# First adaLN columns of a hybrid decoder layer: sums kept in PSUM, wider loads of w_ada, the first gate products in three parts

## The chip, the cores and the metric

The kernel runs on one core of a Trainium2 chip. The core has TensorE (matrix products, PE in the profile), VectorE (DVE), ScalarE (ACT), GpSimd (POOL) and SyncE (SP, which here issues the DMAs), a scratch memory SBUF, and PSUM, the memory that TensorE writes into. The metric is the device time of one execution in microseconds, as the median of several runs.

## The reference

One decoder layer for 1024 tokens of width 1024, in float32. A conditioning vector c gives six vectors (adaLN), the first two of which shift and scale the normed input; the result h is projected, and the projection feeds everything that follows.

```python
mod = jnp.dot(jax.nn.silu(c), w_ada) + b_ada
shift1, scale1, gate1, shift2, scale2, gate2 = [m[:, None, :] for m in jnp.split(mod, 6, axis=-1)]
h = _rmsnorm(x, norm1_w) * (1.0 + scale1) + shift1
proj = jnp.dot(h, w_in)        # queries, keys, values, indexer, retention, two gates ga and gb
...                            # sparse attention and retention, merged by the gates; FFN; last norm
merged = jax.nn.sigmoid(ga) * y_a + jax.nn.sigmoid(gb) * y_r
```

w_ada is 1024 x 6144, w_in is 1024 x 7240, x is 1024 x 1024.

## The kernel before

Every product in float32 is made of three products on TensorE: each operand is split into a high part (rounded to float32r) and a low part (the rest), and high x high, high x low and low x high are added up in PSUM. For a weight, ScalarE makes the high part (`whi`, line 77) and GpSimd the low part (`wlo`, line 80) out of the loaded tile (`graw` or `wraw`).

What the change touches is the **start** of the kernel, about its first 80 us, up to line 321. It works on column blocks of 128, of which there are eight (`KT`), numbered j, and on the first 512 of the 1024 tokens (half 0). For a block j:

1. `load_wa(j)` (line 242) loads the 128 columns j of shift1 and the 128 of scale1 out of w_ada, as two DMAs of 512 KB, into `wa` (three buffers). Each piece that lies together in memory has 128 floats, that is 512 bytes. `rows_slot` (line 95) loads and splits the two tiles `graw` of gb weights that block j needs (six buffers).
2. `start_mod(j)` (line 287) multiplies by silu(c) and adds up over the eight row tiles k, on VectorE: one `tensor_scalar` (line 296) and seven `scalar_tensor_tensor` (line 298), each over 256 columns, which all read and write `acc` in SBUF. Two products with a column of ones (line 302, two instructions each in the trace) add over the partitions into a PSUM tile `mp`, and VectorE makes the two columns `modc` from it (lines 303 and 304).
3. `make_h(j, 0)` (line 272) turns the normed x into columns by four transposes on TensorE (line 275) into a PSUM tile `tp`; ScalarE makes `hT_hi` and `hx` from it with `modc` as scale and bias (line 279), and GpSimd `hT_lo` (line 280).
4. 18 products of 128x512 on TensorE: six PSUM tiles of gb (`gb_ps`) times three kinds (lines 136, 138 and 140: whi x hT_hi, whi x hT_lo, wlo x hT_hi).

PSUM tiles `mp` and `tp` come from one pool of two (`ps_tr`, line 210). Before all that, `norm_x` (line 233) norms each tile of x: a square with a sum on ScalarE (line 236), a power on GpSimd (line 186) and a multiplication on VectorE (line 238), four tiles at the beginning and four, of the second half of the tokens, later. After the eight blocks follow `make_h` for the second half of the tokens, the stores of the gate, and at line 377 eight tiles of the indexer's key weights (`wraw`, 292 columns), whose product with all of hT is the first work that needs all eight blocks (line 123, 128x292).

The instructions of an engine run in the order in which they stand in its queue, each when what it waits for has come. A scheduler makes that order from the program; `turns_after` and `add_manual_dep` add an order to it. SP's queue of DMA issues is kept in order too, so a load that waits for its buffer holds up those behind it.

## Time and profile before

| | us |
|---|---|
| runs (three) | 1731.92, 1732.92, 1734.29 |
| median | 1732.92 |
| the profiled execution: its span, from first to last instruction | 1733.6 |
| TensorE busy in it | 1686.5 (97%) |
| TensorE busy from 0 to 20.5 us | 3.12 |
| TensorE busy from 20.5 to 81.4 us | 50.84 of 60.9 |
| first product of the indexer's keys (line 123) | at 81.45 |

No time beside the span is given for the profiled execution; the span lies between the runs. In the profile an engine's row in the timeline has the start, the duration, engine, line, operation, output<-inputs, shapes and the count of instructions merged into it, and in brackets the idle time before it with what ended it. A row with x6 covers six instructions. Ends of products on TensorE are modelled, so the time from one start to the next says more than a duration. PEclk is the granted clock of TensorE as a share of full speed.

### The profile page before, as it was taken

How to read it: one execution, taken by the hardware profiler on the slowest of the kernel's cores; microseconds unless marked ns; L12 is line 12 of the kernel's file. 1: busy time of each engine (PE TensorE's matmuls, PEld its weight loads, DVE VectorE, ACT ScalarE, POOL GpSimd, SP SyncE). 2: the span in 40 equal slices, each digit the busy share in tenths (PEclk: the TensorE clock that was granted, in tenths of full speed). 3: DMA queues.
4: the chain of work that ended last, by engine and by line, in shares of the span. 5: the costliest groups of instructions: out<-in, count | busy, mean ns of one | idle time of the engine just before them, and what ended most of it. 6: DMA issues, size and time to landing. Idle time of an engine off the chain costs nothing.

```text
span 1733.6 us, 24584 instructions
## 1 busy us (share of the span) xinstructions
PE 1686.5 (97%) x8266; PEld 1394.6 (80%) x8266; DVE 1229.7 (71%) x2118; ACT 755.4 (44%) x1469; POOL 866.6 (50%) x855
## 2 busy tenths in 40 slices
PE   4899999999999999999999999999999999999998
PEld 3797878878888887888777888888888888888887
DVE  7627888898996578765576666975666556687774
ACT  3625643333553444430577246633333333444544
POOL 4553266594533678130346640055554554666674
PEclk9899999999999999999999999999999999999999
DMA  9535523613333356864852740044445444586652
GB/s 279 162 90 172 165 65 112 189 41 83 107 116 116 107 162 200 266 187 154 203 133 72 251 170 1 26 133 152 164 131 187 161 152 141 180 299 200 220 170 97
DMA packets 179486, 260.71 MB, mean 150 GB/s; under 512 B 13520, under 2 KB 111264, under 8 KB 177056
## 3 DMA queue, kind: packets, MB, share of 16 engines
q1 hardware_dynamic: 179216, 258.88, 47.3%
q8 instruction: 65, 1.06, 0.3%
q14 instruction: 61, 0.50, 0.1%
q10 hardware_dynamic: 144, 0.26, 0.0%
HBM read 192.51 MB, written 66.58 MB: 149 GB/s over the span
## 4 chain that ended last, share of the span: by engine, by line
PE 84%; DVE 6%; issue 3%; POOL 3%; DMA 3%; ACT 1%; SPq 0%; POOLq 0%; DVEq 0%; ACTq 0%
PE ya L856 4%; PE ya L854 4%; PE ya L858 4%; PE mm L123 4%; PE mm L126 4%; PE mm L125 4%; PE yb L858 3%; PE yb L854 3%; PE yb L856 3%; PE ya L1683 3%; PE ya L1682 3%; PE ya L1681 3%; PE pva L1199 3%; PE mm L858 2%; PE tra L1178 2%
## 5 line engine op out<-in xcount | busy, mean ns | idle before, releaser
L80 POOL TENSOR_TENSOR wlo<-wraw,whi 128x512 fp32r<-128x512 f32 (+1 forms) x100 | 131.4, 1325 | 139.9 <-ACT whi L77 86.3
L466 DVE TENSOR_SCALAR_CACHE_REDUCE eq<-score,cand 128x384 uint8<-128x384 f32 (+2 forms) x192 | 180.9, 942 | 4.0
L769 POOL TENSOR_TENSOR flo<-tmp,fhi 128x512 fp32r<-128x512 f32 x79 | 108.3, 1371 | 138.9 <-ACT fhi L768 97.5
L123 PE MATMUL mm<-whi,hT_hi 128*128 128x512 f32 (+1 forms) x432 | 163.8, 383 | 1.9 <-ACT qk L657 1.8
L126 PE MATMUL mm<-whi,hT_lo 128*128 128x512 f32 (+1 forms) x432 | 161.8, 376 | 0.0
L125 PE MATMUL mm<-wlo,hT_hi 128*128 128x512 f32 (+1 forms) x432 | 160.9, 374 | 0.0
L854 PE MATMUL ya<-hc,fhi 128*128 128x512 f32 x344 | 133.8, 390 | 1.4 <-DVE c L837 1.4
L856 PE MATMUL ya<-hc,fhi 128*128 128x512 f32 x344 | 134.0, 389 | 0.6 <-DVE hc L1318 0.6
L858 PE MATMUL ya<-hc,flo 128*128 128x512 f32 x344 | 132.9, 389 | 0.0
L1657 ACT ACTIVATE dslot<-draw 128x512 fp32r<-128x512 f32 x143 | 84.4, 627 | 92.3 <-DMA draw<-act_d 35.6
L769 POOL TENSOR_TENSOR flo<-raws,fhi 128x512 fp32r<-128x512 f32 x60 | 86.5, 1448 | 74.5 <-ACT fhi L768 38.1
L1658 POOL TENSOR_TENSOR dslot<-draw,dslot 128x512 fp32r<-128x512 f32 x62 | 96.6, 1576 | 49.4 <-ACT dslot L1657 40.2
L1658 DVE TENSOR_TENSOR dslot<-draw,dslot 128x512 fp32r<-128x512 f32 x81 | 86.0, 1095 | 45.9 <-ACT dslot L1657 45.7
L77 ACT ACTIVATE whi<-wraw 128x512 fp32r<-128x512 f32 (+1 forms) x100 | 58.6, 600 | 102.2 <-DMA wraw<-in_w_in_dram 41.6
L768 ACT ACTIVATE fhi<-tmp 128x512 fp32r<-128x512 f32 x82 | 51.5, 629 | 111.7 <-PE ya L856 58.0
L854 PE MATMUL yb<-hc,fhi 128*128 128x512 f32 x256 | 99.6, 389 | 0.0
L856 PE MATMUL yb<-hc,fhi 128*128 128x512 f32 x256 | 99.6, 389 | 0.0
L858 PE MATMUL yb<-hc,flo 128*128 128x512 f32 x256 | 99.4, 389 | 0.0
L822 DVE TENSOR_TENSOR tmp<-raws 128x512 f32<-128x512 f32 x40 | 31.7, 795 | 86.0 <-POOL flo L769 86.0
L123 PEld LDWEIGHTS mm<-whi,hT_hi 128*128 128x128 f32 x432 | 81.5, 189 | 13.6 <-ACT qk L657 2.2
L126 PEld LDWEIGHTS mm<-whi,hT_lo 128*128 128x128 f32 x432 | 81.4, 189 | 12.6
L1167 POOL TENSOR_SCALAR sx<-sx,mx 128x128 f32<-128x128 f32 (+7 forms) x64 | 47.7, 751 | 87.0 <-DVE mx L1166 65.4
(421 smaller groups left out, 4986.1 us busy)
## 6 DMA issues: line engine op xcount, KB each, us to landing
draw<-act_d SPq DMA_DIRECT2D x70, 256.0 KB
mw<-in_w_ada_dram SPq DMA_DIRECT2D x32, 512.0 KB
act_d<-c SPq DMA_DIRECT2D x58, 256.0 KB
raw<-in_w_in_dram SPq DMA_DIRECT2D x26, 512.0 KB
raws<-in_w_ffn_gate_dram SPq DMA_DIRECT2D x24, 512.0 KB
raws<-in_w_ffn_up_dram SPq DMA_DIRECT2D x24, 512.0 KB
dw<-in_w_ffn_down_dram SPq DMA_DIRECT2D x22, 512.0 KB
dw_d<-dw SPq DMA_DIRECT2D x10, 1024.0 KB
```

Source lines behind the costliest of these rows:

```text
L77: ins = nc.scalar.activation(hi[:, :n], raw[:, :n], AF.Copy)
L80: low = nc.gpsimd.tensor_sub(lo[:, :n], raw[:, :n], f32(hi[:, :n]))
L123: ins = nc.tensor.matmul(ps, lhsT=ahi, rhs=whi[:, :n], start=(i == 0), stop=False)
L125: nc.tensor.matmul(ps, lhsT=ahi, rhs=wlo[:, :n], start=False, stop=False)
L126: nc.tensor.matmul(ps, lhsT=alo, rhs=whi[:, :n], start=False, stop=(i == last))
L466: ins = [nc.vector.tensor_scalar(eq[:, :sc.shape[1]], sc, thr[j], None, op0=op, op1=ALU.add, accum_out=cnt[:, j:j + 1]) for j, sc in enume ...
L769: return ins, (eng or nc.gpsimd).tensor_sub(lo, src, f32(hi))
L854: mm = nc.tensor.matmul(ps, lhsT=whi[:, k, :], rhs=hhi[:, k, :], start=own and k == 0, stop=False, skip_group_check=True)
L856: nc.tensor.matmul(ps, lhsT=whi[:, k, :], rhs=hlo[:, k, :], start=False, stop=False, skip_group_check=True)
L858: nc.tensor.matmul(ps, lhsT=wlo[:, k, :], rhs=hhi[:, k, :], start=False, stop=k == 3, skip_group_check=True)
L1657: nc.scalar.activation(slot[:, 0], raw, AF.Copy)
L1658: ins = lo_eng.tensor_sub(slot[:, 1], raw, f32(slot[:, 0]))
```

## The change

- The columns are summed in groups: (0), (1), (2,3), (4,5), (6), (7). A group has four loads: two halves of the rows (`kh`) times shift and scale. A pair's pieces are 256 floats, that is 1024 bytes, wide. `wa` has two buffers of twice the width in place of three.
- The running sum is kept in a PSUM tile (`acc_ps`, one of the two tiles of `ps_tr`, held until the last group): all but the last addition go to PSUM, the last one goes to `acc` in SBUF. A pair's operations have 512 columns. `mp` and `tp` take turns in the other tile until then.
- The 18 products of a block are made in three parts of six: whi x hT_hi, then wlo x hT_hi, then whi x hT_lo. Between the first and the second the next group's loads and sums are issued, between the second and the third the next block's `make_h`.
- The x tiles 0 to 3 are loaded ahead of the first w_ada columns; x tiles 4 to 7 stand behind the last w_ada load, and so do the loads of the indexer's key weights, whose code is moved up ahead of the second half.
- `sq`, which is written and not read, is bfloat16.

```diff
-    def rows_slot(pieces, kt, n=H, scale=None, low_behind=None, raw=None):
+    def rows_slot(pieces, kt, n=H, scale=None, low_behind=None, raw=None, load_behind=None):
...
+            if load_behind is not None:
+                turns_after(last_load[0], load_behind)
...
+    GROUPS = ((0,), (1,), (2, 3), (4, 5), (6,), (7,))
...
-            tc.add_manual_dep(ins.ins, wa_ins[6].ins.name, NOSYNC, reason="modulation first")
+            tc.add_manual_dep(ins.ins, wa_ins[KT - 1].ins.name, NOSYNC, reason="modulation first")
...
-        sq = start.tile([P, D], F32, name="sq", bufs=1)
+        sq = start.tile([P, D], BF16, name="sq", bufs=1)
...
-    def load_wa(j):
-        was[j] = start.tile([P, 2, KT, P], F32, name="wa", bufs=3)
-        for m in range(2):
-            wa_ins[j] = nc.sync.dma_start(
-                out=was[j][:, m],
-                in_=w_ada[:, m * D + j * P:m * D + (j + 1) * P].rearrange("(k p) n -> p k n", p=P))
+    def load_wa(g):
+        n = len(g) * P
+        wa = was[g] = start.tile([P, 2, KT, 2 * P], F32, name="wa", bufs=2)
+        for kh in range(2):
+            for m in range(2):
+                c0 = m * D + g[0] * P
+                wa_ins[g[-1]] = nc.sync.dma_start(
+                    out=wa[:, m, 4 * kh:4 * kh + 4, :n],
+                    in_=w_ada[kh * H:(kh + 1) * H, c0:c0 + n].rearrange("(k p) n -> p k n", p=P))
...
-    load_wa(0)
     for t in range(4):
         load_x(t)
...
-    for t in range(4):
-        norm_x(t)
...
+    acc_ps = ps_tr()
...
-    def start_mod(j):
-        if j:
-            load_wa(j)
-        wa = was.pop(j)
...
-        acc = start.tile([P, 2, P], F32, name="acc", bufs=2)
+    def start_mod(g):
+        n = len(g) * P
+        wa = was.pop(g)
+        sums = acc_ps[:, :2 * n].rearrange("p (m n) -> p m n", m=2)
+        acc = start.tile([P, 2, 2 * P], F32, name="acc", bufs=1)
         for k in range(KT):
+            src = wa[:, :, k, :n]
+            to = sums if k < KT - 1 else acc[:, :, :n]
             if k == 0:
-                nc.vector.tensor_scalar(acc, wa[:, :, k, :], silu_c[:, k:k + 1], None, op0=ALU.mult)
+                nc.vector.tensor_scalar(to, src, silu_c[:, k:k + 1], None, op0=ALU.mult)
             else:
-                nc.vector.scalar_tensor_tensor(acc, wa[:, :, k, :], silu_c[:, k:k + 1], acc,
-                                               op0=ALU.mult, op1=ALU.add)
+                nc.vector.scalar_tensor_tensor(to, src, silu_c[:, k:k + 1], sums, op0=ALU.mult, op1=ALU.add)
         mp = ps_tr()
...
+    def gb_step(j, part):
+        hhi, hlo = hT.rhs(j, (0,))[0]
+        for i in range(NG):
+            o = (i % 3) * P
+            whi, wlo = (w[:, o:o + P] for w in start_slots[j][i // 3])
+            w, h = ((whi, hhi), (wlo, hhi), (whi, hlo))[part]
+            nc.tensor.matmul(gb_ps[i], lhsT=w, rhs=h, start=j == 0 and part == 0, stop=j == KT - 1 and part == 2)
+
+    start_loads(GROUPS[0])
+    start_loads(GROUPS[1])
+    for t in range(4):
+        norm_x(t)
+    start_mod(GROUPS[0])
+    make_h(0, 0, nc.gpsimd)
+    groups = list(GROUPS[1:])
     for j in range(KT):
-        start_mod(j)
-        make_h(j, 0, nc.gpsimd)
-        for i in range(NG):
...
+        gb_step(j, 0)
+        if groups and groups[0][0] == j + 1:
+            g = groups.pop(0)
+            if groups:
+                start_loads(groups[0])
+            start_mod(g)
+        gb_step(j, 1)
+        if j + 1 < KT:
+            make_h(j + 1, 0, nc.gpsimd)
+        gb_step(j, 2)
+    ik_slots = [rows_slot([(w_in, C_IQ + IQK, IQK)], k, IQK, load_behind=wa_ins[KT - 1]) for k in range(KT)]
...
-    slots = [rows_slot([(w_in, C_IQ + IQK, IQK)], k, IQK) for k in range(KT)]
+    slots = ik_slots
```

Two places of the new order are spoken of below. The lines in the rows are those of the file that each row belongs to: after the change, 313 is the product with ones (302 before), 278 the transposes (275), 325 all 18 products (136 to 140), 308 and 306 the sums (298 and 296), 315 and 316 the two `modc` operations (303 and 304), 187 and 241 the norm of x (185 and 238). A row with xN stands for N instructions.

TensorE's queue before, from the end of one block to the products of the next, in the middle of the eight (`one,acc` goes into `mp`, `ident,x_t` into `tp`; both are tiles of the pool `tr`; `mm` and `lg` are the six gate tiles):

```order
L138 MATMUL lg<-hT_lo_120,whi 128x512
L140 MATMUL lg<-hT_hi_119,wlo 128x512
L136 MATMUL mm<-hT_hi_119,whi 128x512 x3
L136 MATMUL lg<-hT_hi_119,whi 128x512 x3
L302 MATMUL tr<-one,acc 128x1 x2
L275 MATMUL tr<-ident,x_t 128x128 x4
L138 MATMUL mm<-hT_lo_120,whi 128x512
L140 MATMUL mm<-hT_hi_119,wlo 128x512
```

The next block's transposes (L275) stand ahead of twelve products of the block before it (L138 and L140, six of each, of which the first two are shown). After the change, from the transposes for block 2 on:

```order
L278 MATMUL tr<-ident,x_t 128x128 x4
L325 MATMUL mm<-hT_hi_119,whi 128x512 x3
L325 MATMUL lg<-hT_hi_119,whi 128x512 x3
L325 MATMUL mm<-hT_hi_119,wlo 128x512 x3
L325 MATMUL lg<-hT_hi_119,wlo 128x512 x3
L278 MATMUL tr<-ident,x_t 128x128 x4
L325 MATMUL mm<-hT_lo_120,whi 128x512 x3
L325 MATMUL lg<-hT_lo_120,whi 128x512 x3
```

For block 2, as for blocks 1, 4 and 6, the transposes now stand behind all products of the block before, with none of them left between the transposes and the products that need their result (for block 6 only `mp` and the transposes of block 7); for block 3 (the second L278 row), as for 5, six products lie between, and for block 7 all of block 6's.

VectorE's queue before, from the last block's sum to the last `modc` (`ms` and `x_t` belong to the norms of the x tiles 6 and 7):

```order
L296 TENSOR_SCALAR acc<-wa,colT 128x256
L298 SCALAR_TENSOR_TENSOR acc<-wa,colT,acc 128x256
L238 TENSOR_SCALAR x_t<-x_t,rstd 128x1024
L185 TENSOR_SCALAR ms<-ss 128x1
L298 SCALAR_TENSOR_TENSOR acc<-wa,colT,acc 128x256 x5
L238 TENSOR_SCALAR x_t<-x_t,rstd 128x1024
L298 SCALAR_TENSOR_TENSOR acc<-wa,colT,acc 128x256
L303 TENSOR_TENSOR modc<-tr,colT 128x2
L304 SCALAR_TENSOR_TENSOR modc<-modc,colT 128x1
```

The norms stand in among the sum, and the sum of the block before is finished ahead of it. After the change, from the last addition of group (6) to the `modc` of block 6:

```order
L308 SCALAR_TENSOR_TENSOR acc<-wa,colT,tr 128x2x128
L316 SCALAR_TENSOR_TENSOR modc<-modc,colT 128x2
L306 TENSOR_SCALAR tr<-wa,colT 128x256
L308 SCALAR_TENSOR_TENSOR tr<-wa,colT,tr 128x256 x6
L187 TENSOR_SCALAR ms<-ss 128x1
L241 TENSOR_SCALAR x_t<-x_t,rstd 128x1024
L187 TENSOR_SCALAR ms<-ss 128x1 x2
L241 TENSOR_SCALAR x_t<-x_t,rstd 128x1024 x2
L187 TENSOR_SCALAR ms<-ss 128x1
L241 TENSOR_SCALAR x_t<-x_t,rstd 128x1024
L315 TENSOR_TENSOR modc<-tr,colT 128x2
```

All four norms of the second half now stand behind group (7)'s first seven operations and ahead of block 6's `modc` (the last row).

## The prediction

> **What bounds the kernel now.** I read the page's slices first, then the busy time by stage.

> ```profile
> PE   4899999999999999999999999999999999999998
> PEclk9899999999999999999999999999999999999999
> ...
> 0.00:20.50 20.50, 3.12 (x9) 1.76 (x9) 10.10 (x25) 7.72 (x14) 5.05 (x12) 1.00 0.89 279
> 20.50:81.40 60.90, 50.84 (x216) 41.00 (x216) 48.56 (x77) 29.15 (x53) 37.91 (x35) 0.89 0.67 195
> ```

> TensorE is full everywhere but in the first two slices. So a gain here is time taken off the start, up to the first product that needs all eight blocks. From 20.5 to 81.4 TensorE stands for 10 of 60.9 us, and its granted clock (third number from the end) is 0.89. Who makes it stand is in the chain of waits of the first 200 us and in the waits of TensorE between 20.5 and 81.4:

> ```profile
> by line: DVE acc L298 16.9%; issue 9.0%; PE mm L123 7.2%; PE mm L125 7.0%; PE mm L126 6.9%; DMA wraw<-in_w_in_dram 6.3%; POOL wlo L80 4.6%; PE lg L427 3.8%; PE lg L428 3.5%; DVE score L435 3.1%; DMA wa<-in_w_ada_dram 2.7%; DVE acc L296 2.5%
> ...
> PE tr L302 <- DVE acc L298: 8.9, 3, 3.7
> ```

> It is VectorE's sum over w_ada. Why the sum is slow, its instructions show (min/median/max in ns), with the timeline of VectorE and, below, of GpSimd:

> ```profile
> L298 DVE SCALAR_TENSOR_TENSOR acc<-wa,colT,acc x56: 477/485/1514, 8.9 to 70.5; 128x256 f32<-128x256 f32 x56
> ...
> 8.95 2.05 DVE L298 SCALAR_TENSOR_TENSOR acc<-wa,colT,acc 128x256 f32<-128x256 f32 x4
> 31.72 8.68 DVE L298 SCALAR_TENSOR_TENSOR acc<-wa,colT,acc 128x256 f32<-128x256 f32 x7
> ...
> 32.91 3.52 POOL L80 TENSOR_TENSOR wlo<-graw,whi 128x384 fp32r<-128x384 f32 x3
> 36.39 1.46 POOL L280 TENSOR_TENSOR hT_lo<-hx,hT_hi 128x512 fp32r<-128x512 f32 x1
> ```

> Four additions took 2.05 us while GpSimd was idle, seven took 8.68 us while it worked without a break: 0.51 against 1.24 us each. The waits have a second price, seen in the clock and in the starts of products:

> ```profile
> 40.00:44.00 4.00, 3.55 (x13) 3.16 (x14) 3.89 (x9) 0.87 (x2) 1.25 (x2) 0.51 0.60 174
> 72.00:76.00 4.00, 3.98 (x15) 3.31 (x16) 0.32 (x2) 2.39 (x4) 1.04 (x2) 0.50 0.29 75
> ...
> 20.53 1.65 PE L136 MATMUL mm<-hT_hi,whi 128*128 128x512 f32 x3 [0.87 <-ACT hT_hi L279]
> 27.50 0.50 PE L302 MATMUL tr<-one,acc 128*128 128x1 f32 x4
> 42.07 0.78 PE L138 MATMUL mm<-hT_lo,whi 128*128 128x512 f32 x1
> 47.15 0.86 PE L136 MATMUL mm<-hT_hi,whi 128*128 128x512 f32 x3
> 48.55 0.50 PE L302 MATMUL tr<-one,acc 128*128 128x1 f32 x4
> 48.91 0.63 PE L275 MATMUL tr<-ident,x_t 128*128 128x128 f32 x4
> 49.30 0.48 PE L138 MATMUL mm<-hT_lo,whi 128*128 128x512 f32 x1
> 52.12 0.84 PE L136 MATMUL mm<-hT_hi,whi 128*128 128x512 f32 x3
> 53.49 0.50 PE L302 MATMUL tr<-one,acc 128*128 128x1 f32 x4
> 80.57 1.03 PE L275 MATMUL tr<-ident,x_t 128*128 128x128 f32 x8
> 81.45 0.40 PE L123 MATMUL mm<-whi,hT_hi 128*128 128x292 f32 x1
> ```

> Twelve products take 5.08 us from 42.07 (0.42 each) and 2.82 us from 49.30 (0.235 each). After a long gap the clock is half for some 5 us, as it is at the beginning.

> **TensorE's account before.** A full round at full speed is 48.55 to 53.49, 4.94 us. Eight rounds are 39.5; the first block's `mp` and transposes lie before 20.53 (minus 0.75, from 48.55 to 49.30), and four groups of second-half transposes come on top (0.4 each, from 48.91 to 49.30): 40.4 us of work. From 20.53 to 81.45 are 60.9 us, so 20.5 us are lost to waits and half speed. The change can win part of these.

> **Part one: the sums.** Each addition now has one input in SBUF and one in PSUM. The nearest rows are operations of VectorE with one PSUM input, among them ones of a stage in which GpSimd makes low parts all the time:

> ```profile
> L837 DVE TENSOR_TENSOR c<-c,yb x44: 673/678/689, 1119.8 to 1513.3; 128x512 f32<-128x512 f32 x44
> L706 DVE SCALAR_TENSOR_TENSOR rst<-rst,rscale,lg x24: 445/472/484, 292.5 to 460.6; 128x256 f32<-128x256 f32 x24
> L1032 DVE SCALAR_TENSOR_TENSOR stage<-tr,colT,stage x8: 737/744/750, 748.3 to 767.5; 128x512 f32<-128x512 f32 x8
> ```

> Not one of the 44 took over 0.69 us. So I take 0.48 (256 columns) and 0.75 us (512), plus 0.04 between two: about 4.0 us for a single block, 6.2 for a pair. No row shows VectorE writing PSUM. The lower end is these prices (a gain below them has no row), the upper end today's, up to 1.24; I take the lower, since all three rows with a PSUM input lie close together whatever GpSimd does, and weigh the upper as a rival.

> **Part two: the loads.** The rate goes with the length of the pieces: w_ada alone (512 bytes), gate weights (1536) among w_ada, and x (4096):

> ```profile
> GB/s 394 368 343 342 304 292 290 289 289 306 331 383 356 345 314 289 290 298 290 289 321 343 391 381 370 330 313 296 292 288 289 293 289 298 321 352 400 381 349 347
> ...
> DMA packets 317, 1.16 MB, mean 416 GB/s; under 512 B 34, under 2 KB 37, under 8 KB 316
> ...
> 8.56 0.35 DVE L296 TENSOR_SCALAR acc<-wa,colT 128x256 f32<-128x256 f32 x1 [4.18 <-DMA wa<-in_w_ada_dram]
> 23.08 1.02 ACT L77 ACTIVATE whi<-graw 128x384 fp32r<-128x384 f32 x2 [1.11 <-DMA graw<-in_w_in_dram]
> ```

> That is 290, 390 and 416 GB/s. A straight line through the time per piece at 512 and 4096 bytes gives 354 for 1024 bytes, an estimate. A single block (1.05 MB) then takes 3.6 us and a pair (2.1 MB) 5.9 instead of 7.2. The first block was there at 8.5, so data flow from 4.9. In the new order x is in at 9.9, group (0) at 13.5, (1) at 18.1 behind two gate tiles of 0.5 each, six gate tiles until 21.1, (2,3) at 27.0, (4,5) at 33.9, (6) at 40.5, (7) at 44.1, three key weights at 45.3, x tiles 4 to 7 from 46.6 to 50.3. With the sums behind their loads, in VectorE's order, group (2,3) is summed at 31, (4,5) at 38, (6) at 44.5. TensorE, by the account below, asks for them at 33, 43 and 55. So the sums leave the path, and TensorE is next.

> Loading x first costs 3.6 us of w_ada, but not the start: five high parts now stand ahead of the first hT_hi on ScalarE, the fifth of a gate tile that lands at 19.6. With 0.5 for it and 0.9 to TensorE (next fence) the first product starts at 21.0, 0.5 later than before.

> **Part three: the order.** Whether TensorE then stands is decided by what lies between transposes and products:

> ```profile
> 32.54 0.60 PE L275 MATMUL tr<-ident,x_t 128*128 128x128 f32 x4
> 33.17 0.78 ACT L279 ACTIVATE hT_hi<-tr,modc 128x512 fp32r<-128x512 f32 x1 [0.36 <-PE tr L275]
> 30.13 0.78 ACT L279 ACTIVATE hT_hi<-tr,modc 128x512 fp32r<-128x512 f32 x1 [6.02 <-DVE modc L304]
> 31.07 0.94 PE L136 MATMUL mm<-hT_hi,whi 128*128 128x512 f32 x3
> 9.73 1.06 ACT L236 ACTIVATE sq<-x_t 128x1024 f32<-128x1024 f32 x1 [5.10 <-DMA x_t<-in_x_dram]
> 11.96 0.75 DVE L238 TENSOR_SCALAR x_t<-x_t,rstd 128x1024 f32<-128x1024 f32 x1
> ```

> From transposes to ScalarE are 0.63, from there to the product 0.94, together 1.57; less the transposes' own 0.4, a gap of 1.2. It comes for blocks 1, 2, 4 and 6, whose transposes stand straight ahead of their products: 4.8. Before, twelve products covered it. For blocks 3 and 5 six products (1.4) cover it, but ahead of block 5's hT_hi stand three squares of x on ScalarE (1.06 plus 0.2 for the sum's read; the third can end at 51.1): 0.8 more. New gaps: 5.6. With one `tr` tile left, `mp` waits for ScalarE's reading of `tp` and `tp` for VectorE's of `mp`; both are over when TensorE comes there, since 12 products lie between. `sq` in bfloat16 and the additions' last step into SBUF I put at nothing: as many columns as before, and behind ScalarE's and VectorE's slack; without it, some tenths.

> **The sum.** TensorE after: work 40.0 (one group of second-half transposes fewer stands ahead of the key products), half speed in the first round 2.8 (20.53 to 27.50 took 6.97 for 18 products, 4.2 at 0.235), gaps 5.6: 48.4 from 21.0, so 69.4 instead of 81.45. That is 12.0 won, 0.4 given back by the group that comes later: 11.6. From some 50 us behind that place on, all five queues have the same order as before, so it should carry to the end. The span would be 1733.6 - 11.6 = 1722.0. The span is 0.7 over the median of the runs, and I take the difference from that: **1732.9 - 11.6 = 1721.3 us**.

> **Rivals.**

> *The norms hold up block 6.* All four norms stand ahead of block 6's `modc`. The last x is in at 50.3, and its square can start behind block 5's two conversions at 52.6. From the start of a square to the end of its norm are 3.0 us (9.73 to 12.71 in the fence above), so 55.6; TensorE wants `modc` at 57. Any delay beyond 1.4 us passes through, and so does the fourth key weight, whose high part stands ahead of hT_hi(6) on ScalarE and whose load waits for a GpSimd step behind the last norm's power. I price it at 3 to 7 us: 1724 to 1728, chance 0.18. [...]

> *The change doesn't do what it says:* additions into PSUM stay as slow as today beside GpSimd, whose mix of work gives them a mean of 0.72 us (groups by line: busy us, mean ns):

> ```profile
> L298 DVE SCALAR_TENSOR_TENSOR acc<-wa,colT,acc 128x256 f32<-128x256 f32 x56 | 40.1, 716 | 1.5
> ```

> With 1.43 for 512 columns 32 short and 16 long operations last 46 us instead of 28 (4 times 4.0 and twice 6.2). They start at 13.5 and share VectorE with 4 us of norms, so they end near 64, and the last block's queue of 10.5 us of work follows (36 products of blocks 6 and 7 at 0.235, 8.5 us, with transposes and `mp`). The first key product comes at 74.5: 6.5 us won, 1726.4; chance 0.08.

> *Slower: half speed all through.* If gaps of 1.2 us already halve the clock, a product costs 0.42 instead of 0.235: 0.19 times 126 products in rounds two to eight is 24 us, and the time 1732.9 + 12.4 = 1745. It decides from 61 products on (11.6 / 0.19). Against it:

> ```profile
> 63.12 0.86 PE L136 MATMUL lg<-hT_hi,whi 128*128 128x512 f32 x3
> 64.95 0.50 PE L138 MATMUL mm<-hT_lo,whi 128*128 128x512 f32 x1 [0.98 <-POOL hT_lo L280]
> ```

> This gap of one microsecond left the products behind it at 0.39 each. [...] Chance 0.04.

> *No difference:* new waits of over 8 us in queues that I have read only for order, 1731; chance 0.07.

> **Chances.** The forecast, 1715.5 to 1724: 0.60. Below it, all gaps covered (11.6 + 5.6 + 0.5 won, 1715.2): 0.03. Then the rivals. The range 1715.5 to 1728 takes the forecast and the two rivals that still win; 0.14 is left out. A measurement of this kernel tells 0.2% (3.5 us) from nothing: faster 0.89, same 0.07, slower 0.04.

> **What would show it.** Right: additions of at most 0.55 us (256) and 0.8 us (512) beside a busy GpSimd; no wait of TensorE for the sum over 1 us after 30 us; PEclk 1.00 between 30 and 70 us; the first 128x292 product near 69.4. Wrong in part: gaps of TensorE over 2 us before blocks 5 to 7 with ScalarE or VectorE's norms as the releaser; wide loads at 290. Wrong altogether: additions over 1 us, a clock near 0.5 behind 30 us, or the first key product past 80.

## The result, and the profile after

The changed kernel takes 1721.9 us (median of 4 runs, 1720.92 to 1723.81); the kernel before, on the same chip, 1732.42 us (4 runs, 1730.5 to 1734.29). The ratio is 0.9941, 95% interval 0.9928 to 0.9954. The forecast was 1721.3 us, in a range from 1715.5 to 1728. In a second measurement, on another occasion, the changed kernel took 1722.52 us against 1733.71, a ratio of 0.9935 (0.9922 to 0.9948).

The page's slices of the profiled execution (span 1721.0 us), and its start by stage (the columns are as in the rows shown of before: length, busy time of PE, PEld, DVE, ACT and POOL, PEclk, DMA share, GB/s):

```profile
PE   5999999999999999999999999999999999999998
PEclk9999999999999999999999999999999999999999
```

```profile
20.50:69.40 48.90, 42.65 (x204) 34.60 (x205) 26.21 (x53) 27.02 (x49) 33.44 (x34) 1.00 0.77 241
20.50:81.40 60.90, 54.65 (x297) 46.49 (x298) 29.27 (x58) 35.48 (x63) 35.08 (x36) 1.00 0.80 252
```

From 20.5 to 81.4 us TensorE is busy 54.65 us instead of 50.84, at a clock of 1.00 instead of 0.89, and in this time it now runs 297 instructions instead of 216. (In neither kernel does this column show the half speed of the first round: three products take 1.65 us at 21.17 and 0.96 at 29.83.) VectorE is down from 48.56 to 29.27 us. What TensorE still waits for (us in total, times, longest), and its timeline at the start of each block:

```profile
PE mm L325 <- ACT hT_hi L282: 7.0, 5, 2.1
PE tr L278 <- DVE modc L315: 0.3, 1, 0.3
```

```profile
21.17 1.65 PE L325 MATMUL mm<-hT_hi,whi 128*128 128x512 f32 x3 [1.63 <-ACT hT_hi L282]
29.83 0.96 PE L325 MATMUL mm<-hT_hi,whi 128*128 128x512 f32 x3 [1.74 <-ACT hT_hi L282]
36.43 0.97 PE L325 MATMUL mm<-hT_hi,whi 128*128 128x512 f32 x3 [0.87 <-ACT hT_hi L282]
48.82 0.98 PE L325 MATMUL mm<-hT_hi,whi 128*128 128x512 f32 x3 [2.07 <-ACT hT_hi L282]
60.75 0.96 PE L325 MATMUL mm<-hT_hi,whi 128*128 128x512 f32 x3 [0.65 <-ACT hT_hi L282]
70.33 0.38 PE L125 MATMUL mm<-whi,hT_hi 128*128 128x292 f32 x1
```

No wait for the sum is left; every gap ahead of a block now ends with `hT_hi` from ScalarE. The first key product starts at 70.33 us; before it was 81.45. VectorE's additions in groups by form (busy us, mean ns, idle us ahead of them and its releaser):

```profile
L308 DVE SCALAR_TENSOR_TENSOR tr<-wa,colT,tr 128x256 f32<-128x256 f32 x24 | 11.7, 489 | 0.7
L308 DVE SCALAR_TENSOR_TENSOR tr<-wa,colT,tr 128x512 f32<-128x512 f32 x12 | 9.1, 756 | 0.3
L306 DVE TENSOR_SCALAR tr<-wa,colT 128x512 f32<-128x512 f32 x2 | 1.5, 754 | 4.0 <-DMA wa<-in_w_ada_dram 4.0
```

All 36 additions into PSUM together took 20.8 us. It is now VectorE that waits for the loads. The same span of the DMA queues from 5 to 25 us, in slices of 0.5 us:

```profile
GB/s 418 418 451 401 401 401 426 442 358 330 343 297 290 292 292 299 325 371 334 296 291 287 294 289 290 323 363 375 375 369 381 353 367 340 350 354 342 350 344 352
```

One reads x first (over 400), then two single blocks (290) with gate weights between, then the first pair of blocks with its pieces of 1024 bytes (340 to 354).

### The profile page after: what moved, and what is told of

It reads as the page before. It is cut to its first block, busy times and chain, and to the rows that moved or that the text cites. A ratio compares the mean times of both kernels' runs of the same rounds, so it can differ in the third digit from the quotient of the medians.

```text
span 1721.0 us, 24561 instructions
## 1 busy us (share of the span) xinstructions
PE 1677.6 (97%) x8266; PEld 1388.6 (81%) x8266; DVE 1208.7 (70%) x2098; ACT 755.6 (44%) x1469; POOL 862.1 (50%) x855
## 3 DMA queue, kind: packets, MB, share of 16 engines
q8 instruction: 65, 1.06, 0.3%
## 4 chain that ended last, share of the span: by engine, by line
PE 86%; issue 3%; DVE 3%; DMA 3%; POOL 2%; ACT 1%; SPq 1%; POOLq 0%; DVEq 0%; ACTq 0%
PE ya L888 4%; PE ya L886 4%; PE ya L890 4%; PE mm L125 4%; PE mm L128 4%; PE mm L127 4%; PE yb L888 3%; PE yb L890 3%; PE yb L886 3%; PE ya L1715 3%; PE ya L1713 3%; PE pva L1231 3%; PE ya L1714 3%; PE mm L890 2%; PE tra L1210 2%
## 5 line engine op out<-in xcount | busy, mean ns | idle before, releaser
L80 POOL TENSOR_TENSOR wlo<-wraw,whi 128x512 fp32r<-128x512 f32 (+1 forms) x100 | 130.0, 1310 | 139.8 <-ACT whi L77 86.4
L125 PE MATMUL mm<-whi,hT_hi 128*128 128x512 f32 (+1 forms) x432 | 163.7, 383 | 1.9 <-ACT qk L689 1.8
L77 ACT ACTIVATE whi<-wraw 128x512 fp32r<-128x512 f32 (+1 forms) x100 | 58.7, 601 | 116.5 <-DMA wraw<-in_w_in_dram 39.2
L125 PEld LDWEIGHTS mm<-whi,hT_hi 128*128 128x128 f32 x432 | 81.1, 188 | 13.4 <-ACT qk L689 2.2
```

The costliest lines, as they stand in the source:

```text
L77: ins = nc.scalar.activation(hi[:, :n], raw[:, :n], AF.Copy)
L80: low = nc.gpsimd.tensor_sub(lo[:, :n], raw[:, :n], f32(hi[:, :n]))
L125: ins = nc.tensor.matmul(ps, lhsT=ahi, rhs=whi[:, :n], start=(i == 0), stop=False)
```

## The experiments

Experiments 1 to 4 take the change apart, 5 to 11 try the gaps that are left. A theory is what is expected if the explanation holds, a rival what is expected if another one does. The table crosses the parts; each ratio is to the kernel before on the same chip (medians 1732.4 to 1733.9), and "key product" is the start of the first 128x292 product in the profiled execution.

| PSUM sums | wide loads, x first | new order | kernel | key product | median, us | ratio to before |
|---|---|---|---|---|---|---|
| no | no | no | before | 81.45 | 1732.42 | 1 |
| yes | no | no | experiment 1 | 71.36 | 1723.52 | 0.9944 (0.9931 to 0.9956) |
| no | yes | yes | experiment 2 | 85.93 | 1735.81 | 1.0015 (1.0006 to 1.0024) |
| yes | x first only | yes | experiment 3 | 78.33 | 1728.22 | 0.9963 (0.9949 to 0.9977) |
| yes | yes | no | experiment 4 | 73.18 | 1729.70 | 0.9983 (0.9971 to 0.9995) |
| yes | yes | yes | the change | 70.33 | 1721.90 | 0.9941 (0.9928 to 0.9954) |

**1. The PSUM sum alone, in the kernel before.**

```diff
+        sums = acc_ps[:, :2 * P].rearrange("p (m n) -> p m n", m=2)
...
+            to = sums if k < KT - 1 else acc
...
-                nc.vector.scalar_tensor_tensor(acc, wa[:, :, k, :], silu_c[:, k:k + 1], acc,
+                nc.vector.scalar_tensor_tensor(to, wa[:, :, k, :], silu_c[:, k:k + 1], sums,
```

`acc_ps` is one `tr` tile that is kept for all blocks, as in the change.

> The kernel before with one part of the change alone: the running sum over w_ada stays in PSUM, with single blocks, the old loads and the old order of the products. Theory (the sum is slow because VectorE's additions from SBUF run beside GpSimd, and the PSUM sum cures that by itself): additions of 256 columns at about 0.49 us whatever GpSimd does, no wait of TensorE for the sum over 1 us behind 30 us, TensorE at full clock there. Each round still has the transposes straight ahead of its products (some 6 gaps of 1.2 us) and may wait for a low part, so the first key product comes near 73.5 us (20.5 + 40.4 work + 2.8 half speed + 7 gaps + 3 low parts), and the time is near 1724.5 us (1723 to 1727). Rival (the loads and the order carry the gain, or PSUM additions are no cheaper beside GpSimd): 1731 to 1733 us.

Measured: 1723.52 us, the whole gain of the change. Its additions, and TensorE's starts and waits:

```profile
L301 DVE SCALAR_TENSOR_TENSOR tr<-wa,colT,tr 128x256 f32<-128x256 f32 x48 | 23.4, 488 | 1.3
```

```profile
19.57 1.65 PE L136 MATMUL mm<-hT_hi,whi 128*128 128x512 f32 x3 [0.87 <-ACT hT_hi L279]
28.56 0.99 PE L136 MATMUL mm<-hT_hi,whi 128*128 128x512 f32 x3 [0.87 <-ACT hT_hi L279]
50.33 0.50 PE L138 MATMUL mm<-hT_lo,whi 128*128 128x512 f32 x1 [0.60 <-POOL hT_lo L280]
```

488 ns each, in the old order and with GpSimd at work: the theory holds. In the kernel before, the 28 additions that ran while GpSimd was idle took 479 to 486 ns, and the 28 beside an operation of GpSimd 948 ns on average, up to 1514. In the changed kernel the 17 additions of 256 columns into PSUM that ran beside GpSimd took 490 ns each, the 7 others 481 to 490; those of 512 columns took 756 ns, six beside GpSimd and six not. The first key product comes at 71.36 us, 2.1 us sooner than expected. The kernel starts 1.6 us sooner than the changed kernel (w_ada's first block comes ahead of x, and only one block's high parts stand ahead of the first hT_hi) and has short gaps of 0.87 us.

**2. The change without the PSUM sum.**

```diff
+    nc.vector.memset(acc_ps, 0.0)
...
-        sums = acc_ps[:, :2 * n].rearrange("p (m n) -> p m n", m=2)
         acc = start.tile([P, 2, 2 * P], F32, name="acc", bufs=1)
+        sums = acc[:, :, :n]
...
-            to = sums if k < KT - 1 else acc[:, :, :n]
+            to = sums
```

The `memset` runs once and only keeps the PSUM tile allocated.

> The changed kernel with one part undone: the running sum is in SBUF again (the PSUM tile stays allocated, so the tr buffers are as in the changed kernel); loads and order as changed. Theory: additions go back to a mean of 0.72 us or more (256 columns) and 1.4 to 2.4 us (512) beside GpSimd, VectorE's sums last 46 us or more instead of 28, TensorE waits for them again, the first key product comes at 74.5 us or later, and the time is near 1728 us (1725 to 1733). Rival (wider additions, loads in time and the new order have taken the sum off the path whatever its price): 1721 to 1723 us.

Measured: 1735.81 us, above the theory's range (its upper end was 1733) and slower than before.

```profile
L309 DVE SCALAR_TENSOR_TENSOR acc<-wa,colT,acc 128x256 f32<-128x256 f32 x28 | 21.5, 768 | 0.8
L309 DVE SCALAR_TENSOR_TENSOR acc<-wa,colT,acc 128x512 f32<-128x512 f32 x14 | 15.2, 1082 | 0.4
```

```profile
74.50 0.98 PE L314 MATMUL tr<-one,acc 128*128 128x1 f32 x4 [2.63 <-DVE acc L309]
```

The same additions took 768 ns and 1082 ns instead of 489 and 756 (for 512 columns the theory said 1.4 us or more). TensorE waits for the sum again, and the first key product comes at 85.93 us. So the loads and the order win nothing by themselves here; experiments 1 and 2 together show that the sum's place carries the gain.

**3. The change with single blocks:** `GROUPS = tuple((j,) for j in range(KT))`.

> The changed kernel with all eight blocks of w_ada in groups of their own (pieces of 512 bytes, additions of 256 columns); sums in PSUM and the new order stay. Theory (TensorE is the bound, the sums have slack): the two pairs cost 2.6 us more of loading at 290 instead of 345 GB/s, so the second half of x is in 2.6 us later; the sums are still done ahead of TensorE's asking; the time is 1722.9 us (1721.5 to 1725), the delay through the norms ahead of the last blocks' modc. Rival (the wide transfers carry a good part of the gain): 1726 us or more.

Measured: 1728.22 us. It lies above the theory's range; the rival got the time, but not by its cause. ScalarE and TensorE ahead of block 5, and the clock behind it:

```profile
56.99 1.06 ACT L239 ACTIVATE sq<-x_t 128x1024 bf16<-128x1024 f32 x1 [1.83 <-DMA x_t<-in_x_dram]
58.05 0.76 ACT L282 ACTIVATE hT_hi<-tr,modc 128x512 fp32r<-128x512 f32 x1
```

```profile
58.86 1.65 PE L325 MATMUL mm<-hT_hi,whi 128*128 128x512 f32 x3 [5.11 <-ACT hT_hi L282]
```

```profile
60.00:64.00 4.00, 4.00 (x11) 3.13 (x10) 1.32 (x4) 3.48 (x8) 2.16 (x3) 0.50 0.05 18
```

A square of a later x tile stands ahead of block 5's hT_hi on ScalarE, and its tile landed only at 57 us: 5.11 us of gap, and half speed behind it.

**4. The change with the old order of products** (a block's eighteen products behind its transposes, `mm_ch_step` as before).

> The changed kernel with the gate products of a block issued as before (all of a block behind its transposes, low parts straight behind the first six products) and the next sum behind them; PSUM sums and loads stay. Theory: the low part of h is asked for 1.4 us earlier in each round, behind six products instead of twelve, so TensorE waits some 0.3 to 0.6 us for GpSimd in most of eight rounds, and the time is near 1725 us (1723 to 1728). Rival (the three parts are worth nothing, or cost what the new gaps cost): 1719 to 1722 us.

Measured: 1729.70 us over 9 runs that spread from 1725.85 to 1732.91; the theory's range ended at 1728. No wait for a low part shows, so the theory's cause is wrong, though its sign was right. What costs is again ScalarE's queue, ahead of block 4:

```profile
48.65 1.06 ACT L239 ACTIVATE sq<-x_t 128x1024 bf16<-128x1024 f32 x1 [0.73 <-DMA x_t<-in_x_dram]
49.70 0.76 ACT L282 ACTIVATE hT_hi<-tr,modc 128x512 fp32r<-128x512 f32 x1
```

```profile
50.52 1.28 PE L138 MATMUL mm<-hT_hi,whi 128*128 128x512 f32 x3 [3.20 <-ACT hT_hi L282]
```

The profiled execution is the fastest of the nine; its key product is 2.9 us late and its time 4.0 us above the changed kernel's median. Where the other eight lost up to 7 us more is not shown.

**5. Single blocks, ScalarE's queue freed.** The kernel of experiment 3 with

```diff
-        nc.scalar.activation(sq, xt[t], AF.Square, accum_out=ss)
+        ins = nc.scalar.activation(sq, xt[t], AF.Square, accum_out=ss)
+        if t >= 4:
+            turns_after(ins, h_ins[6])
...
-    ik_slots = [rows_slot([(w_in, C_IQ + IQK, IQK)], k, IQK, load_behind=wa_ins[KT - 1]) for k in range(KT)]
+    ik_slots = [rows_slot([(w_in, C_IQ + IQK, IQK)], k, IQK, load_behind=wa_ins[KT - 1],
+                          behind=h_ins[5]) for k in range(KT)]
```

`h_ins[j]` is the second conversion of block j; `behind` is handed on to the high part.

> The changed kernel with single blocks, as in the experiment before (median 1728.2), and ScalarE's queue ordered at two places, computing the same: the squares of the second half of x stand behind block 6's conversions, the key weights' high parts behind block 5's. Theory (single blocks cost time only because the later x tiles are waited for by a square that stands ahead of block 5's hT_hi on ScalarE, 5.1 us, and because that gap halves the clock for 6 us more): no gap over 2 us ahead of block 5, full clock from 25 us on, and the time is near 1724 us (1722 to 1726). Rival (the slower loads themselves are the cost): 1727 to 1729 us as without the order.

Measured: 1725.49 us (ratio 0.9960, 0.9948 to 0.9972; runs from 1722.87 to 1732.68). The place behaves as the theory says: block 5 starts at 54.46 behind 0.87 us of gap instead of at 58.86 behind 5.11, and the key product at 71.35 instead of 78.33. The times of experiments 3 and 5 overlap, so of the 7 us won there the end shows at most a part. The profiled execution is the slowest of the ten runs; where it lost time behind the key product is not shown.

**6. Four buffers for single blocks:** the `wa` tile has one block's width and `bufs=4`.

> The changed kernel with single blocks again, but with four buffers of one block for w_ada instead of two buffers of two (the same bytes of SBUF). Theory (what single blocks cost is not the shorter piece of 512 bytes but that two buffers let only two blocks be on the way, so that the loads stand while VectorE sums: x tile 4 was waited for till 57 us with two buffers): the loads run without a break, the second half of x is in near 51 us, and the time is 1722.5 us (1721 to 1724.5). Rival (the wide transfers are what counts): 1725 us or more.

Measured: 1731.23 us (0.9989, 0.9980 to 0.9998). ScalarE could start on the second half of x at 51.2 us as expected (57.0 in experiment 3), and still the theory fails: three gaps of 2.62, 2.25 and 2.32 us come up, two of them with half speed behind them. Ahead of hT_hi on ScalarE stand high parts of gate tiles that are still on their way (the first two gaps) and the square of x tile 4 (the third). The width of the pieces cannot be told from the order that comes with it.

**7. Idle transposes ahead of the start:** 32 transposes of an x tile from 10.56 us on, ahead of the first `mp`.

> The changed kernel with 32 more transposes (128x128, of the second x tile, into a bank that the first product overwrites; nobody reads them) ahead of the first block's column sums, so that TensorE works from about 10.4 to 16.5 us. It adds work and leaves nothing out. Both theories expect the first round at full clock (18 products at 0.235 us instead of 6.3 us for the round). Theory (the chain to block 1 does not run through TensorE: its hT_hi stands on ScalarE behind two gate tiles that land at 28.05 us): the first round ends 2.5 us sooner, TensorE stands that much longer ahead of block 1, which starts at 29.8 us as before, and the time stays at 1721.9 us (1720.9 to 1723.5; slower if the longer gap of some 4 us lowers the clock again). Rival (the prediction's term of 2.8 us for the half speed of round one is a cost on the path): 1719.1 us.

Measured: 1722.53 us (ratio 0.9941, 0.9929 to 0.9953). The time is the one that the theory gave, but by itself it proves nothing, for the premise of theory and rival failed:

```profile
18.30 0.66 PE L278 MATMUL tr<-ident,x_t 128*128 128x128 f32 x4 [0.50 <-DVE modc L315]
21.25 1.39 PE L325 MATMUL mm<-hT_hi,whi 128*128 128x512 f32 x3 [2.30 <-ACT hT_hi L282]
```

```profile
22.00:24.00 2.00, 2.00 (x6) 1.60 (x5) 0.00 (x0) 1.10 (x3) 2.00 (x3) 0.50 1.11 350
```

The transposes did raise the clock (four of them take 0.66 us at 18.3; in the changed kernel 1.12 at 18.42), but behind the wait of 2.30 us for ScalarE it was low again, and round one was about as slow as ever. Block 1 starts at 29.92 as in the changed kernel. A second stretch at half speed, from 48.9 to 52.3 us behind a gap of 1.83 us ahead of block 4, puts the key product at 71.31. What the half speed of round one is worth is answered below by the two profiles of the changed kernel ("The sum").

**8. Two queues ordered by hand.** ScalarE: each gate block's high parts behind the conversions of the block before. TensorE: `mp` behind part 0, the transposes behind part 1, each instruction in the turn of the one ahead of it:

```diff
-        start_slots[j] = [rows_slot(
+    def start_split(j, behind=None):
+        start_slots[j] = [split_weight(raw, 3 * P, behind=behind) for raw in start_raws.pop(j)]
...
+    def step(ins):
+        if steps:
+            turns_after(ins, steps[-1])
+        steps.append(ins)
...
+            h_ins[j + 1] = make_h(j + 1, 0, nc.gpsimd)
+            if j + 2 < KT:
+                start_split(j + 2, behind=h_ins[j + 1])
```

> The changed kernel with two queues ordered by hand, computing the same. ScalarE: the high parts of a gate block stand behind the conversions of the block before it, the key weights' behind block 4's. TensorE: the column sums of a group stand behind the first six products of the block before, the transposes behind the next six, the last six cover ScalarE. Theory (after the change the path runs through ScalarE's queue, where high parts that wait for loads stand ahead of hT_hi): the first product comes at 19.3 instead of 21.17 us, the gaps ahead of blocks 1, 4 and 6 (1.7, 2.1, 0.65) shrink to 0.3 or so, in their place TensorE waits up to 2.6 us for the sum of group (2,3), done at 30.9; block 4 starts near 44.6 instead of 48.8, the first key product near 66 to 67, the time is 1717.8 us (1716 to 1720.5). Rival (the gaps are set by the loads and by VectorE, and only change their name): 1721 to 1723 us.

Measured: 1725.76 us (0.9957, 0.9945 to 0.9970), above both expectations; all its runs are slower than those of experiment 7 on the same chip.

```profile
31.16 1.02 PE L329 MATMUL tr<-one,acc 128*128 128x1 f32 x8 [2.12 <-DVE acc L324]
51.98 0.96 PE L341 MATMUL mm<-hT_hi,whi 128*128 128x512 f32 x3 [1.90 <-ACT hT_hi L284]
69.01 0.66 PE L278 MATMUL tr<-ident,x_t 128*128 128x128 f32 x4 [1.22 <-ACT hx L284]
70.35 0.66 PE L278 MATMUL tr<-ident,x_t 128*128 128x128 f32 x4 [0.68 <-ACT hx L284]
72.26 0.61 PE L125 MATMUL mm<-whi,hT_hi 128*128 128x292 f32 x1 [1.25 <-ACT gstage L272]
```

The gaps ahead of blocks 1, 4 and 6 are gone and the wait for group (2,3) came as expected. A gap of 1.90 us ahead of block 5 is new; it ends with hT_hi from ScalarE, which in the changed kernel stands behind three squares of x (49.3 to 52.8 us). And at the end of the stage TensorE waits 3.2 us for the second half's conversions and for the sigmoid that frees a bank, all on ScalarE, and the key products run at half speed (0.44 us against 0.29). The rival's account is nearer, though its time was too low: what was won changed its name.

**9. The same with the idle transposes** of experiment 7.

> The kernel with the ordered queues and the 32 idle transposes together. Theory (with the queues ordered, the next thing on the path is the sum of group (2,3), which its load allows at 30.9 us): round one ends 2.5 us sooner and TensorE waits that much longer for the sum, so the time is that of the ordered queues alone, within 1 us (about 1718 us). Rival (with ScalarE's queue freed the half speed of round one is on the path): 2 to 3 us less than the ordered queues alone.

Measured: 1725.69 us (0.9959, 0.9947 to 0.9972), as the theory says:

```profile
19.78 0.96 PE L341 MATMUL mm<-hT_hi,whi 128*128 128x512 f32 x3 [0.87 <-ACT hT_hi L284]
31.08 1.02 PE L329 MATMUL tr<-one,acc 128*128 128x1 f32 x8 [3.04 <-DVE acc L324]
```

Here round one runs at full clock (0.96 us for three products, not 1.65), and TensorE then waits 3.04 instead of 2.12 us for a sum that comes at 31.1 us in both. The key product comes 2 us sooner (70.22 instead of 72.26), and the time is the same.

**10. Ordered to the end of the stage,** with single blocks in four buffers, the squares behind block 5 and

```diff
+            if hf == 1 and j >= 1:
+                turns_after(ins, sig_ins[2])
...
+            if len(sig_ins) == 1:
+                turns_after(sig_ins[0], keys_high)
```

> The kernel with the ordered queues, and four things more, computing the same: single blocks in four buffers; the squares of the second half of x behind block 5's conversions; all key weights' high parts ahead of the first sigmoid on ScalarE; the second half's conversions from block 1 on behind the third sigmoid. Theory (the ordered queues were 2 us ahead at the end of block 7 and lost it where TensorE waited 3.2 us for ScalarE's conversions and sigmoid, at half speed behind that; the cause is the order of ScalarE's queue again): no wait for the sum of block 2, none over 2 us behind it, full clock from 28 us on, the first key product at 63 to 65 us, and the time is near 1717 us (1714 to 1721). Rival (whatever is won ahead of the key products is lost at the end of the stage, because the second half of x sets it): 1722 to 1726 us.

Measured: 1732.13 us (0.9989, 0.9980 to 0.9997); the theory's number is missed by 15 us. Behind the first product, blocks 0 to 5 ran without one gap, as it said; ahead of block 6 there are two, of 1.78 and 1.39 us. At the end the order itself did harm: the sigmoids stand behind key weights that are still being loaded and behind a table load of ScalarE (1.28 us), and TensorE waits for the bank they free:

```profile
72.01 0.40 PE L125 MATMUL mm<-whi,hT_hi 128*128 128x292 f32 x1 [4.11 <-ACT gstage L276]
```

**11. One turn moved:** in the changed kernel only the key weights' high parts go behind block 4's conversions (`behind=h_ins[4]`).

> The changed kernel with one edit to the order of ScalarE, computing the same: the high parts of the key weights stand behind block 4's conversions instead of ahead of them. Theory (the gap ahead of block 4 was 2.07 us instead of the predicted 1.2 because three key weights' high parts, 1.3 us, stand ahead of its hT_hi): the gap is 0.9 us, block 4 starts at 47.6 instead of 48.8, and the first key product comes 1.0 to 1.4 us sooner, at 69.1; the time is 1720.8 us (1719.5 to 1722.5), too near to the changed kernel's to tell by time alone. Rival (the high parts only fill a wait that the transposes set): gap and block 4 as before, 2.1 us and 48.8.

Measured: 1723.28 us (0.9940, 0.9925 to 0.9955), with the changed kernel itself (experiment 12) on the same chip:

> The changed kernel itself, on the chip of the run beside it, to have its time under the same conditions: 1721.9 us as measured before, 1720.5 to 1723.5.

```profile
47.62 0.96 PE L326 MATMUL mm<-hT_hi,whi 128*128 128x512 f32 x3 [0.87 <-ACT hT_hi L282]
59.69 0.66 PE L278 MATMUL tr<-ident,x_t 128*128 128x128 f32 x4 [1.54 <-DVE modc L316]
71.25 0.38 PE L125 MATMUL mm<-whi,hT_hi 128*128 128x292 f32 x1
```

```profile
58.28 1.28 DVE L241 TENSOR_SCALAR x_t<-x_t,rstd 128x1024 f32<-128x1024 f32 x1 [0.58 <-POOL rstd L188]
59.48 0.15 DVE L316 TENSOR_TENSOR modc<-tr,colT 128x2 f32<-128x2 f32 x1
```

At its place the theory is right: the gap is 0.87 and block 4 starts at 47.62 (48.82 and 48.78 in the two profiles of the changed kernel). The 1.2 us are gone again eleven us later: TensorE reaches the last `modc` ahead of VectorE, which is still at the last norm, stands 1.54 us, and the clock is at half from 60.4 to 63.9 us. So the key product is late instead of early (71.25 us, 69.1 expected), and the time lies above the theory's range. This is the prediction's rival of the norms, seen at work.

None of these versions is faster than the changed kernel; experiments 1, 7 and 11 are level with it within their intervals.

## Why the prediction was right

**The bound, and part one.** Right, and shown by experiments 1 and 2 from both sides. The prices of 0.48 and 0.75 us, taken from operations of VectorE with one PSUM input in other stages, measured 0.489 and 0.756. An addition of 256 columns took 768 ns with both inputs in SBUF (experiment 2) and 489 with one in PSUM (the changed kernel), in nearly the same order beside the same work of GpSimd; and while GpSimd was idle, 485 with both in SBUF (the kernel before). So the rival that PSUM additions are no cheaper is out. By what mechanism an addition with both inputs in SBUF is slow beside GpSimd, no run shows.

**Part two.** The dates held: the sums of (2,3), (4,5) and (6) were foretold for 31, 38 and 44.5 us; on VectorE's timeline they end at 30.9, 37.95 and 45.4. Pieces of 1024 bytes ran at some 345 GB/s; the estimate was 354 (the line through 290 and 416 GB/s gives 351). What the prediction didn't see is that the gain needs none of this: experiment 1 has it with the old loads and the old order.

**Part three.** The sum of the new gaps was right by luck of its parts. Foretold were 1.2 us each ahead of blocks 1, 2, 4 and 6 and 0.8 ahead of block 5, in all 5.6. Measured were 1.74, 0.87, 2.07 and 0.90 (0.65 and 0.25 for `modc`) and none ahead of block 5: 5.58. The price itself was too high: where nothing stands in the way a gap is 0.87 us. Blocks 1 and 4 were above it because high parts stand ahead of hT_hi on ScalarE:

```profile
28.05 1.06 ACT L77 ACTIVATE whi<-graw 128x384 fp32r<-128x384 f32 x2 [5.03 <-DMA graw<-in_w_in_dram]
29.01 0.76 ACT L282 ACTIVATE hT_hi<-tr,modc 128x512 fp32r<-128x512 f32 x1
46.79 1.30 ACT L77 ACTIVATE whi<-wraw 128x292 fp32r<-128x292 f32 x3 [5.00 <-PE tr L278]
48.00 0.76 ACT L282 ACTIVATE hT_hi<-tr,modc 128x512 fp32r<-128x512 f32 x1
```

Experiment 11 shows it for block 4: with the three key weights moved the gap is 0.87. (What releases the three key weights is not shown: the row names TensorE, and in experiment 4, where they start at 46.61 us, it names their load.) The prediction used this mechanism for the first product (21.0 foretold, 21.17 measured) but didn't look for it at the later blocks.

**The sum.** From the first product to the first key product 48.4 us were foretold, 49.16 measured (70.33 less 21.17); so the key product came 0.93 us later than the 69.4 foretold, of which 0.17 lie in the start and the rest in work and half speed (43.6 instead of 42.8). At that place 11.1 us were won instead of 12.0. But half speed and gaps don't add up as the sum has it. The second profile of the changed kernel (experiment 12), from the transposes for block 1 on, shows it:

```profile
28.77 0.60 PE L278 MATMUL tr<-ident,x_t 128*128 128x128 f32 x4
30.23 0.96 PE L325 MATMUL mm<-hT_hi,whi 128*128 128x512 f32 x3 [0.87 <-ACT hT_hi L282]
48.78 0.96 PE L325 MATMUL mm<-hT_hi,whi 128*128 128x512 f32 x3 [1.62 <-ACT hT_hi L282]
70.38 0.38 PE L125 MATMUL mm<-whi,hT_hi 128*128 128x292 f32 x1
```

Here half speed lasts longer, and the transposes for block 1 come 1.3 us later than in the first profile (27.49). Block 1 starts 0.4 us later, block 4 and the key product at the same times within 0.05 us: the gaps ahead of blocks 1 and 4 are 0.87 and 1.62 us instead of 1.74 and 2.07. So the half speed of round one, 2.8 us in the sum, is no cost of its own on the path, as far as these 1.3 us show. ScalarE's queue sets when block 4 starts, and the gaps ahead of it take up what TensorE loses or wins before. This speaks for the theory of experiment 7 and against its rival.

**The way to the end.** "It should carry to the end" held: the profiled spans differ by 12.6 us, the medians by 10.5, the gain at the key product is 11.1. That is no law. In experiments 3 to 10, whose orders differ further back, the span less the start of the key product lies between 1648 and 1659 us (before 1652.2, after 1650.7), so their times tell less than the places named with each. The two profiles of the changed kernel alone give 1650.7 and 1648.2.

**The rivals.** Half speed all through did not come: the gaps of the changed kernel, 2.07 us at most, left the clock at 1.00. The norms did not hold up block 6 by more than the 0.25 us for its neighbour's `modc`. The other half of that rival came true in a small way: the fourth key weight's high part stands ahead of hT_hi(6) and waits 1.38 us for its load, and 0.65 us of it reach TensorE at most.

```profile
59.59 0.45 ACT L77 ACTIVATE whi<-wraw 128x292 fp32r<-128x292 f32 x1 [1.38 <-DMA wraw<-in_w_in_dram]
```

Experiment 11 shows that there was no margin: TensorE came 1.2 us sooner and waited 1.3 us longer (1.54 against 0.25). So the chance given to it was earned.

**What stays open:** how much wide loads or the order of products are worth by themselves (every test of them moved ScalarE's queue as well), and why the runs of experiment 4 spread by 7 us.

## What to carry to other kernels

Where VectorE accumulates in SBUF beside a busy GpSimd, try the running sum in PSUM: here this one edit took an addition from 716 to 488 ns on average (before, experiment 1) and gave the ten microseconds. Ahead of an in-order queue ask for each instruction on the path what stands ahead of it and what that waits for; moving it pays only until the next queue is late, and here each of five tries at the remaining gaps (experiments 7 to 11) gained nothing at the end. And test a change of several parts by its parts, in both directions: here two of the three won nothing together without the third, and nothing on top of it, and with one of the two taken back the other did harm.

## What the runs showed of the hardware

```profile
40.08:46.91 6.83, 6.46 (x19) 5.40 (x20) 6.62 (x13) 2.27 (x4) 3.43 (x4) 0.50 0.83 253
70.80:77.62 6.82, 5.97 (x21) 4.94 (x22) 1.70 (x4) 3.23 (x5) 2.50 (x3) 0.50 0.26 67
```

From 40.08 to 70.80 are 30.72 us, nine times 3.413. (The prediction read the half speed behind a long gap as some 5 us.) In the 3.41 us ahead of a fall to half speed TensorE was busy for 0.71 and 0.58 us in the kernel before, not at all in experiment 3, for some 0.5 us in experiment 4 and 1.95 in experiment 2. Ahead of a multiple at which the clock stayed at 1.00, it was busy for at least 2.07 us in the kernel before and 1.59 in the changed one (from 26 to 90 us). With the same 1.59 us the clock stayed in the changed kernel (first row) and fell in experiment 7 (second and third), so this busy time alone does not tell it either:

```profile
45.16:48.58 3.42, 1.59 (x9) 1.09 (x8) 3.22 (x8) 1.77 (x4) 1.26 (x2) 1.00 1.04 383
45.46:48.88 3.42, 1.59 (x10) 1.13 (x9) 3.21 (x9) 2.18 (x5) 1.67 (x3) 1.00 1.04 399
48.88:52.29 3.41, 3.41 (x9) 2.63 (x10) 1.30 (x4) 3.35 (x6) 2.48 (x4) 0.50 0.95 350
```

So a gap cost twice here or only once: gaps of 2.07 (after), 2.14 (before) and 2.25 us (experiment 6) left the clock at 1.00, while 1.54 (experiment 11), 1.83 (experiment 7), 2.32, 3.20 and 5.11 us (experiments 6, 4 and 3) were followed by half speed. In experiment 4 half speed set in when TensorE was at work again (gap from 47.3 to 50.5, half speed from 51.0 to 54.4). As an estimate, half of the measured 3.41 us, a stretch at half speed costs up to 1.7 us on top of the gap. In experiment 7 the clock was up behind the 32 idle transposes: the next four took 0.66 us, in the changed kernel 1.12.

**GpSimd gains too.** Its low parts of 384 columns took 1158 ns on average in the kernel before (20.5 to 81.4 us) and 1012 in the changed one (from 20 to 70 us: 1008 in experiment 1, 1188 in experiment 2). Together with VectorE's additions (948 ns beside GpSimd, 485 without it, in the kernel before) this shows that the two engines slowed each other there.
